# Moving the first attention step in an S5 and cross-attention layer, and joining two exponential and sine chains

## The chip, the cores and the metric

The kernel runs on one core of one Trainium2 chip. The core has a matmul engine (PE, with its weight loads shown as PEld), a vector engine (DVE), an activation engine (ACT), a general engine (POOL) and a queue that issues most DMAs (SP). The metric is the device time of one execution in microseconds (us); less is better.

## The reference

One encoder layer over 2048 tokens of width 1024 (`DEPTH = 1`, so only the S5 mixer is used). One input projection gives 512 columns for the S5 mixer and 256 for the queries of a cross-attention into 256 memory tokens; both results go through one output projection, a layer norm, a mixture of 16 experts and a second norm.

```python
proj = x @ s5_w_in[j]
mix = _s5_mixer(proj[..., :S5_WIDTH], ...)
mem_out = _memory_attention(proj[..., -MEM_WIDTH:], mem, mem_w_kv[i])
y = jnp.concatenate([mix, mem_out], axis=-1) @ w_out
x = _layer_norm(DEEPNORM_ALPHA * x + y, ln1_g[i], ln1_b[i])
moe = _hier_moe(x, ...)
x = _layer_norm(DEEPNORM_ALPHA * x + moe, ln2_g[i], ln2_b[i])
```

The S5 mixer is a diagonal complex state space model in two directions, with 32 groups of 64 states; its result goes through a GELU and a gated linear layer (GLU):

```python
step = jnp.exp(log_step[direction])[:, None]
lam_bar = jnp.exp(lam * step)                    # one token's decay and turn
b_bar = ((lam_bar - 1.0) / lam)[..., None] * bmat
bu = jnp.einsum('blgc,gpc->blgp', ug, b_bar)
_, states = lax.associative_scan(_ssm_combine, (a, bu), reverse=(direction == 1), axis=1)
y = y + jnp.real(jnp.einsum('gcp,blgp->blgc', cmat, states))
g = jax.nn.gelu(y)
return g * jax.nn.sigmoid(g @ w_glu + b_glu)
```

The cross-attention is a softmax over 256 memory tokens for 4 heads of 64.

## The kernel before

The 2048 tokens are cut into 128 chunks of 16. Inside a chunk the S5 mixer is a set of matmuls with tables made from the powers of `lam_bar`; from chunk to chunk runs a scan. The 32 groups are taken in 8 blocks of 4.

**Input projection and tables (`inproj_u`, up to about 243 us).** Sixteen token tiles are projected on PE: `pu` (S5 part) and `pq` (queries), 24 and 48 matmuls a tile. `pq` has one PSUM buffer, which ACT (L294) and DVE (L295, `OT<-pq`) empty, so PE's next `pq` waits for DVE. Beside it `s5_base` makes the token's decay and turn and their powers `PR`, `PI` for 0 to 16 tokens, on DVE and partly on POOL. `exp_m1` is a chain of 16 small DVE instructions, `sincos` one of 23; each works on 64 columns. They run for the step, for a token (`rate`, `th`) and, at the function's end, for a chunk (16 times the rate and the angle). The chunk's results `decay` and `turn` feed `scan_base`, which doubles a table of turns `E` (L649 to L671, the last doublings in three sets of 512 columns). `s5_block` then makes each block's tables on DVE (`wzi`, `wi`, `wzo`, `wo`, L580 and L581) and POOL (`wtmpi`, `wtmpo`, L576), which PE transposes (`ptw`) and multiplies (`pkk`); DVE finishes a block with `ks` (L617).

**Scans (about 229 to 334 us).** `scan(b)` runs on DVE and POOL (L690 to L695, L715), in the order of blocks 6, 7, 0 to 5; ACT copies its result to `SS` (L720). Meanwhile `kv` projects the memory and PE multiplies the chunk inputs (`pvv`).

**Outputs and attention (about 290 to 440 us).** `s5_out(b)` has for each block four pieces of PE work (`py`, L802 to L805), and after every second block four pieces of transposes (`trg`, L816), each followed by `gelu`: ACT squares (L824), DVE (L825), ACT's tanh (L826), DVE (L827, `S<-gu,trg`, which reads `trg` for the last time). `py`, `trg` and `pvv` share three PSUM buffers. Before each piece the generator yields: 4 + 8 in each pair of blocks, 48 in all. There PE may take steps of attention. A token tile of attention is three steps: scores (`pS` on PE, two PSUM buffers; DVE's maximum `nm`, L737; ACT's exponential `pe`, L740; DVE's `ri`, L742; POOL's product, L743), probabilities (`pT`, L757, emptied to `th` and `tl`) and values (`po`, L773). Steps of different tiles are interleaved, 57 in all. PE's order here is written by hand, and the table `STEPS` says how many steps go ahead of each piece. The other engines' order, and PE's elsewhere, is set by the framework's scheduler from its own estimates. Buffers of the attention and of later weights lie where those of the scan lay.

**After it:** the GLU (`gh`, `gl`, `pg`), the output projection with routing, then the experts to the end.

Of the kernel before, what the change touches and what calls it, by code (L numbers as in the profile page):

```python
# [9 lines left out]
F32 = mybir.dt.float32  # L10
# [8 lines left out]
P = 128  # L19
# [4 lines left out]
G = 32  # L24
# [26 lines left out]
SPLIT = 1024  # L51
WHOLE_T = 12
BATCHES = ((0, 4), (4, 4), (8, 2), (10, 2), (12, 2), (14, 2))
STEPS = (0,) * 8 + (1,) + (2,) * 39
ATL = (2, 3)
WIP = 3
LW = 4
# [15 lines left out]
class Kern:  # L73
# [307 lines left out]
    def s5_base(self, t0):  # L381
        nc, a = self.nc, self.a
        bp = t0.enter_context(self.pool("s5b", side="right"))
        N = 2 * G
        V = nc.vector
# [9 lines left out]
        with ExitStack() as s:  # L395
            tp = s.enter_context(self.pool("s5t", side="right"))
            n_t = [0]

            def T(nm, dt=F32):
                n_t[0] += 1  # L400

                ring = {"tag": "poly", "bufs": 3} if nm == "poly" else {}
                return tp.tile([P, N], dt, name=f"b_{nm}{n_t[0]}", **ring)

            def ts(x, s1, op0, s2=None, op1=None, dt=F32):
                o = T("ts", dt)
# [3 lines left out]
            def tt(x, y, op):  # L410
                o = T("tt")
                V.tensor_tensor(o, x, y, op=op)
                return o
# [21 lines left out]
            def exp_m1(x):  # L435
                x = ts(x, -87.0, ALU.max, 88.0, ALU.min)
                n = rnd(x, 1.4426950408889634)
                r = stt(n, -0.693145751953125, x, MUL, ADD)
                r = stt(n, -1.42860682030941723212e-6, r, MUL, ADD)
                q = horner(r, [1 / 40320., 1 / 5040., 1 / 720., 1 / 120., 1 / 24., 1 / 6., 0.5, 1.0])  # L440
                sc = ts(n, 127.0, ADD, 8388608.0, MUL, dt=I32).bitcast(F32)
                m = tt(q, sc, MUL)
                return stt(sc, -1.0, m, ADD, ADD)
# [5 lines left out]
            def sincos(th):  # L449

                n = rnd(th, 1.0 / (2 * math.pi))
                r = stt(n, -6.28125, th, MUL, ADD)
                r = stt(n, -0.0019350051879882812, r, MUL, ADD)
                r = stt(n, -(2 * math.pi - 6.28125 - 0.0019350051879882812), r, MUL, ADD)
                w = ts(r, 0.25, MUL)
                z = tt(w, w, MUL)
                sp = horner(z, [1 / 362880., -1 / 5040., 1 / 120., -1 / 6.])
                s = stt(sp, 1.0, w, ADD, MUL)
                c = ts(horner(z, [-1 / 3628800., 1 / 40320., -1 / 720., 1 / 24., -0.5]), 1.0, ADD)
                s2 = stt(s, 2.0, c, MUL, MUL)  # L460
                c2 = ts(tt(s, s, MUL), -2.0, MUL, 1.0, ADD)
                return stt(s2, 2.0, c2, MUL, MUL), stt(s2, -2.0, s2, MUL, MUL)

            step = ts(exp_m1(lst), 1.0, ADD)
            rate = tt(lre, step, MUL)
            em = exp_m1(rate)
            th = tt(lim, step, MUL)
            sf, cm = sincos(th)
            cf = ts(cm, 1.0, ADD)
            er = tt(tt(em, cf, MUL), cm, ADD)  # L470
            ei = stt(em, 1.0, sf, ADD, MUL)
            PR, PI = self.PR, self.PI
# [30 lines left out]
            for d in range(2):  # L503
                V = (nc.vector, nc.gpsimd)[d]
# [22 lines left out]
            V.tensor_tensor(self.Dd, dcol.unsqueeze(2).to_broadcast([P, NB, 16]),  # L527
                            e32.unsqueeze(1).to_broadcast([P, NB, 16]), op=MUL)

            decay = ts(exp_m1(ts(rate, 16.0, MUL)), 1.0, ADD)  # L530
            sin, cos = sincos(ts(th, 16.0, MUL))
            for par in range(2):
                r = slice(par * 64, par * 64 + 64)
                for d in range(2):
                    col = slice(d * G + par, d * G + G, 2)
                    V.tensor_copy(self.decay[r, :, d], decay[r, col])
                    V.tensor_scalar(self.turn[r, 0, :, d], cos[r, col], 1.0, None, op0=ADD)
                    V.tensor_scalar(self.turn[r, 1, :, d], sin[r, col], 1.0 - 2.0 * d, None, op0=MUL)
        self.dump("PR", self.PR)
        self.dump("PI", self.PI)  # L540
        d = self.dram
# [1065 lines left out]
```

## Time and profile before

| | |
|---|---|
| median of 3 runs | 1087.34 us |
| range | 1083.37 to 1088.72 us |
| the profiled execution | 1077.7 us |
| its span on the core | 1075.9 us |
| PE busy | 896.7 us (83%) |
| DVE busy | 825.0 us (77%) |
| ACT, POOL busy | 540.8, 537.4 us |

The span runs from the core's first to its last instruction; the execution's own time has 1.8 us around it. A share of busy time is a mean over stages with different limits, so the stages are read one by one: for each, which engine never waits, and what the other waits for. In rows of waits, the engine and line that waited stand first, then what ended the wait, then the sum, the count and the longest.

### The profile page before, as it was taken

What the parts mean: (1) busy time and instruction counts of PE and PEld (TensorE: products, weight loads), DVE (VectorE), ACT (ScalarE), POOL (GpSimd) and SP (SyncE); (2) the same over time, 40 slices, a digit from 0 to 9 for tenths busy, and PEclk for the clock granted to TensorE, in tenths of its full rate; (3) what the DMA queues carried; (4) which work ended last, traced back from release to release, by engine and by line L of the source; (5) the groups of instructions that cost most, each with busy time, mean ns of one, the idle gap of its engine ahead of it and who ended that gap; (6) DMA issues with size and microseconds to landing.
All of it is one profiled execution on the core that took longest, in us unless ns stands there. A gap on an engine that the chain in (4) does not pass through costs nothing. (4 is left out here: it accounts for less than half of the span.)

```text
span 1075.9 us, 18762 instructions
## 1 busy us (share of the span) xinstructions
PE 896.7 (83%) x7108; PEld 607.8 (56%) x7108; DVE 825.0 (77%) x1636; ACT 540.8 (50%) x1068; POOL 537.4 (50%) x379
## 2 busy tenths in 40 slices
PE   7778599986754999899999988599959996988980
PEld 4445465675643777444555557486647664755640
DVE  7999988969997676384486866379858787978874
ACT  5122253445748777477743421366636564745530
POOL 1475755426664332324946364524544566357554
PEclk9899899999886999999999996899989999999995
DMA  7113355275171422326755341675568669658431
GB/s 258 40 44 119 122 181 200 70 234 188 48 226 43 154 80 80 120 77 244 252 177 80 121 116 62 246 294 192 199 239 306 214 227 341 216 193 286 170 96 66
DMA packets 65198, 178.14 MB, mean 166 GB/s; under 512 B 15120, under 2 KB 33424, under 8 KB 57680
## 3 DMA queue, kind: packets, MB, share of 16 engines
q1 hardware_dynamic: 44800, 128.83, 36.5%
q0 software_dynamic: 20304, 48.07, 12.9%
q8 instruction: 57, 0.93, 0.4%
q14 instruction: 37, 0.30, 0.1%
HBM read 141.95 MB, written 58.49 MB: 186 GB/s over the span
## 5 line engine op out<-in xcount | busy, mean ns | idle before, releaser
L92 DVE SCALAR_TENSOR_TENSOR wl<-raw,wh 128x1024 f16<-128x1024 f32 x82 | 97.7, 1219 | 10.1 <-ACT wh L91 10.1
L91 ACT ACTIVATE wh<-raw 128x1024 f16<-128x1024 f32 x82 | 82.0, 1048 | 23.3 <-PE pg L109 12.2
L109 PE MATMUL pg<-xl,wh 128*128 128x288 f16 (+1 forms) x256 | 72.4, 285 | 5.1 <-DVE xl L1477 4.4
L108 PE MATMUL pg<-xh,wh 128*128 128x288 f16 (+1 forms) x256 | 72.8, 286 | 2.9 <-ACT xh L1476 1.8
L1221 POOL DMA_INDIRECT xs<-xg,idxall x31 | 39.4, 1272 | 71.4 <-DVE xg L1514 41.9
L108 PE MATMUL pu<-xh,wh 128*128 128x288 f16 (+1 forms) x256 | 72.1, 284 | 1.9 <-DVE hl L1063 1.9
L110 PE MATMUL pg<-xh,wl 128*128 128x288 f16 (+1 forms) x256 | 72.1, 284 | 0.5 <-issue 0.5
L110 PE MATMUL pu<-xh,wl 128*128 128x288 f16 (+1 forms) x256 | 72.0, 284 | 0.0
L109 PE MATMUL pu<-xl,wh 128*128 128x288 f16 (+1 forms) x256 | 71.9, 284 | 0.0
L109 PEld LDWEIGHTS <-wh 128*128 128x128 f16 x576 | 58.1, 101 | 20.6 <-issue 7.1
L110 PEld LDWEIGHTS <-wl 128*128 128x128 f16 x576 | 57.9, 101 | 20.0 <-issue 6.8
L108 PEld LDWEIGHTS <-wh 128*128 128x128 f16 x576 | 58.0, 101 | 19.4 <-issue 4.6
L108 PE MATMUL pq<-xh,S 128*128 128x128 f16 x256 | 50.1, 233 | 15.9 <-DVE OT L295 15.9
L743 POOL TENSOR_TENSOR pe<-pe,ri 128x1024 f32<-128x1024 f32 x16 | 30.3, 1895 | 54.5 <-DVE ri L742 40.6
L108 PE MATMUL py<-wh,hh 128*128 128x512 f16 x120 | 45.9, 384 | 13.2 <-DVE xg L1514 10.1
L1216 POOL DMA_INDIRECT xg<-x1d,idxall x31 | 39.2, 1266 | 32.6 <-DMA out_x<-xg,idxall 14.5
L108 PE MATMUL pu<-winh,xh 128*128 128x512 f16 x128 | 49.7, 389 | 6.7 <-ACT winh L91 6.6
L691 POOL TENSOR_TENSOR m<-S,R 128x1024 f32<-128x1024 f32 x10 | 31.4, 3144 | 41.7 <-DVE S L715 23.6
L110 PE MATMUL pq<-xh,S 128*128 128x128 f16 x256 | 50.3, 233 | 0.0
L109 PE MATMUL pq<-xl,S 128*128 128x128 f16 x256 | 50.1, 233 | 0.0
L1477 DVE TENSOR_TENSOR xl<-pt,xh 128x512 f16<-128x512 f32 x60 | 39.5, 682 | 13.6 <-ACT xh L1476 8.4
L109 PE MATMUL pu<-winl,xh 128*128 128x512 f16 x128 | 49.4, 386 | 0.3 <-DVE winl L92 0.3
(471 smaller groups left out, 3134.1 us busy)
## 6 DMA issues: line engine op xcount, KB each, us to landing
raw<-in_w_gate SPq DMA_DIRECT2D x16, 1024.0 KB
raw<-in_w_up SPq DMA_DIRECT2D x16, 1024.0 KB
raw<-in_w_down SPq DMA_DIRECT2D x16, 1024.0 KB
xr<-in_xT SPq DMA_DIRECT2D x16, 512.0 KB
xs<-wo SPq DMA_DIRECT2D x16, 512.0 KB
wol<-xs SPq DMA_DIRECT2D x16, 512.0 KB
M<-kd SPq DMA_DIRECT2D x64, 128.0 KB
xres<-in_x SPq DMA_DIRECT2D x16, 512.0 KB
```

The costliest lines, as they stand in the source:

```text
L91: self.nc.scalar.activation(hi, raw, AF.Copy, scale=WS)
L92: self.nc.vector.scalar_tensor_tensor(lo, raw, WS, hi, op0=ALU.mult, op1=ALU.subtract)
L108: mm(ps, lh, rh, start=first, stop=False)
L109: mm(ps, lh, rl, start=False, stop=False)
L110: return mm(ps, ll, rh, start=False, stop=last)
L691: Q.tensor_tensor(m[:, 1], S[:, :, 1::-1], tab(1), op=ALU.mult)
L743: nc.gpsimd.tensor_tensor(pe, pe, ri.unsqueeze(2).to_broadcast([P, 4, 256]), op=ALU.mult)
L1216: return self.nc.gpsimd.indirect_dma_start(out=out, out_offset=None, in_=src, in_offset=bass.IndirectOffsetOnAxis(ap=idx, axis=0))
L1221: st = self.nc.gpsimd.indirect_dma_start(out=self.xs, out_offset=bass.IndirectOffsetOnAxis(ap=si, axis=0), in_=z[:sz], in_offset=None, bou ...
L1477: nc.vector.tensor_tensor(xl[:, ds_, :n], pt, xh[:, ds_, :n], op=ALU.subtract)
```

## The change

Two edits. The table `STEPS` now has no attention step in the first 20 places and two in each of the other 28, so the first step stands ahead of the transposes of blocks 2 and 3 instead of at those of blocks 0 and 1, and the last stands at the kernel's last transposes instead of in those of blocks 4 and 5. And `s5_base` puts a token's and a chunk's rate side by side into one tile of 128 columns, their angles likewise, and runs one `exp_m1` and one `sincos` over both; the chunk's own chains at the end of the function are gone.

```diff
-STEPS = (0,) * 8 + (1,) + (2,) * 39
+STEPS = (0,) * 20 + (2,) * 28
@@ s5_base
+            wide = False
             def T(nm, dt=F32):
                 n_t[0] += 1
-                ring = {"tag": "poly", "bufs": 3} if nm == "poly" else {}
-                return tp.tile([P, N], dt, name=f"b_{nm}{n_t[0]}", **ring)
+                ring = {"tag": "poly" + "w" * wide, "bufs": 3} if nm == "poly" else {}
+                return tp.tile([P, 2 * N if wide else N], dt, name=f"b_{nm}{n_t[0]}", **ring)
...
             step = ts(exp_m1(lst), 1.0, ADD)
-            rate = tt(lre, step, MUL)
-            em = exp_m1(rate)
-            th = tt(lim, step, MUL)
-            sf, cm = sincos(th)
-            cf = ts(cm, 1.0, ADD)
+            rates = tp.tile([P, 2 * N], F32, name="rates")
+            ths = tp.tile([P, 2 * N], F32, name="ths")
+            for o, x in ((rates, lre), (ths, lim)):
+                V.tensor_tensor(o[:, 0:N], x, step, op=MUL)
+                V.tensor_scalar(o[:, N:], o[:, 0:N], 16.0, None, op0=MUL)
+            wide = True
+            ems = exp_m1(rates)
+            sfs, cms = sincos(ths)
+            cfs = tp.tile([P, 2 * N], F32, name="cfs")
+            V.tensor_scalar(cfs, cms, 1.0, None, op0=ADD)
+            wide = False
+            em, sf, cm, cf = (x[:, 0:N] for x in (ems, sfs, cms, cfs))
...
-            decay = ts(exp_m1(ts(rate, 16.0, MUL)), 1.0, ADD)
-            sin, cos = sincos(ts(th, 16.0, MUL))
             for par in range(2):
                 r = slice(par * 64, par * 64 + 64)
                 for d in range(2):
-                    col = slice(d * G + par, d * G + G, 2)
-                    V.tensor_copy(self.decay[r, :, d], decay[r, col])
-                    V.tensor_scalar(self.turn[r, 0, :, d], cos[r, col], 1.0, None, op0=ADD)
-                    V.tensor_scalar(self.turn[r, 1, :, d], sin[r, col], 1.0 - 2.0 * d, None, op0=MUL)
+                    col = slice(N + d * G + par, N + d * G + G, 2)
+                    V.tensor_scalar(self.decay[r, :, d], ems[r, col], 1.0, None, op0=ADD)
+                    V.tensor_copy(self.turn[r, 0, :, d], cfs[r, col])
+                    V.tensor_scalar(self.turn[r, 1, :, d], sfs[r, col], 1.0 - 2.0 * d, None, op0=MUL)
```

DVE has 1582 instructions instead of 1622; the other engines' counts stay (PE 12108, ACT 985, POOL 407, SP 304). Line numbers after the edit are 8 to 10 higher in `s5_base` and 8 higher below it. The scheduler also arranges many rows anew.

PE at the first transposes `trg`, before: between the first of them and the next two stand scores `pS` of tile 0 (the last four rows of it are here), and the scores of tile 1 follow.

```order
L734 LDWEIGHTS OT
L734 MATMUL pS_3527<-kh,OT 128x256
L735 LDWEIGHTS OT
L735 MATMUL pS_3527<-kl,OT 128x256
L816 MATMUL trg_3539<-ident,gt_3437 128x128 x4
L816 MATMUL trg_3549<-ident,gt_3437 128x128 x4
L734 LDWEIGHTS OT
L734 MATMUL pS_3561<-kh,OT 128x256
```

PE at the same place now: all four transposes stand together, and the outputs `py` of block 2 follow.

```order
L824 MATMUL trg_3424<-ident,gt_3355 128x128 x4
L824 MATMUL trg_3434<-ident,gt_3355 128x128 x4
L824 MATMUL trg_3444<-ident,gt_3355 128x128 x4
L824 MATMUL trg_3454<-ident,gt_3355 128x128 x4
L810 MATMUL py_3472<-M_3467,U 128x256
L811 MATMUL py_3472<-M_3467,U 128x256
L812 MATMUL py_3472<-wol_3465,SS 128x256
L813 MATMUL py_3472<-wol_3465,SS 128x256
```

Scores have moved behind 32 matmuls `py` of blocks 2 and 3 (8 of these rows are shown above in part), to the next transposes.

ACT at that place, before: `SS` of the last scan (the second row of x8), then the exponentials of tile 0.

```order
L824 ACTIVATE gu_3511<-trg_3506 128x512
L824 ACTIVATE gu_3544<-trg_3539 128x512
L826 ACTIVATE gu_3511<-gu_3511 128x512
L720 ACTIVATE SS<-S 64x2x128 x8
L740 ACTIVATE pe_3516,sm_3517<-pS_3518,nm_3523 128x256 x2
L740 ACTIVATE pe_3516,sm_3517<-pS_3527,nm_3532 128x256 x2
```

ACT now: the last scan's `SS` stands ahead of both tanh (L834), and no exponential is near.

```order
L832 ACTIVATE gu_3429<-trg_3424 128x512
L832 ACTIVATE gu_3439<-trg_3434 128x512
L728 ACTIVATE SS<-S 64x2x128 x8
L834 ACTIVATE gu_3429<-gu_3429 128x512
L834 ACTIVATE gu_3439<-gu_3439 128x512
L832 ACTIVATE gu_3449<-trg_3444 128x512
```

The first tanh has moved behind the last scan's copies.

DVE ahead of the first block's `ks`, before: of the three sets of 512 columns of `E`, one stands ahead of it (L666, L667, L670).

```order
L580 TENSOR_TENSOR wzo_680<-XC,PRb 128x512
L660 TENSOR_TENSOR E<-E,S 128x64
L295 SCALAR_TENSOR_TENSOR OT<-pq_1275,OT 64x2x128
L581 TENSOR_TENSOR wo_645<-wzo_680,wtmpo_675 128x2x256
L666 TENSOR_TENSOR S<-E 128x512
L667 TENSOR_TENSOR S<-E 128x512
L580 TENSOR_TENSOR wzi_906<-XB,PRb 128x2x240
L670 TENSOR_TENSOR E<-S 128x32x16
L581 TENSOR_TENSOR wi_902<-wzi_906,wtmpi_904 128x2x240
L617 TENSOR_TENSOR ks_724<-ks_724,Dd 128x16
```

DVE now, at the block's first `wo`: the second and third set stand there, and its `ks` comes twelve rows after the last row shown.

```order
L588 TENSOR_TENSOR wzo_586<-XC,PRb 128x512
L674 TENSOR_TENSOR S<-E 128x512
L675 TENSOR_TENSOR S<-E 128x512
L589 TENSOR_TENSOR wo_563<-wzo_586,wtmpo_584 128x2x256
L678 TENSOR_TENSOR E<-S 128x32x16
L588 TENSOR_TENSOR wzo_589<-XC,PRb 128x512
L674 TENSOR_TENSOR S<-E 128x512
L675 TENSOR_TENSOR S<-E 128x512
L589 TENSOR_TENSOR wo_563<-wzo_589,wtmpo_584 128x2x256
L678 TENSOR_TENSOR E<-S 128x32x16
```

Two sets of the scan's table have moved ahead of the first block's end.

## Rows read from the trace of the kernel before

**Rows 1.** Engine busy time by stretch: start:end, length, busy (instructions), clock, DMA.
```profile
27.00:54.00 27.00, 20.37 (x151) 13.39 (x150) 26.50 (x101) 4.60 (x8) 13.25 (x15) 0.87 0.14 40
108.00:135.00 27.00, 14.55 (x174) 11.73 (x174) 25.33 (x35) 7.54 (x19) 19.48 (x11) 0.81 0.36 122
162.00:189.00 27.00, 27.00 (x208) 15.72 (x205) 22.52 (x34) 10.13 (x25) 13.72 (x7) 1.00 0.57 203
300.00:330.00 30.00, 13.25 (x48) 9.66 (x48) 28.33 (x35) 14.67 (x35) 19.20 (x7) 0.73 0.70 209
```

**Rows 2.** PE's waits at 30 to 60, 60 to 90 and 90 to 135 us.
```profile
PE pq L108 <- DVE OT L295: 6.6, 2, 4.4
...
PE pq L108 <- DVE OT L295: 7.5, 3, 3.5
...
PE pkk L614 <- DVE wo L581: 7.2, 1, 7.2
```

**Rows 3.** DVE in order of time: start, duration, instruction, count.
```profile
20.24 0.28 DVE L527 TENSOR_TENSOR Dd<-dcol,e 128x128 f32<-128x128 f32 x1
20.44 0.22 DVE L431 SCALAR_TENSOR_TENSOR b_poly<-b_poly,b_st 128x64 f32<-128x64 f32 x1
...
35.83 0.22 DVE L417 SCALAR_TENSOR_TENSOR b_st<-b_st 128x64 f32<-128x64 f32 x1
35.97 0.22 DVE L431 SCALAR_TENSOR_TENSOR b_poly<-b_poly,b_st 128x64 f32<-128x64 f32 x1
...
36.24 0.19 DVE L407 TENSOR_SCALAR b_ts<-b_st 128x64 f32<-128x64 f32 x1
36.34 0.22 DVE L431 SCALAR_TENSOR_TENSOR b_poly<-b_poly,b_st 128x64 f32<-128x64 f32 x1
```

**Rows 4.** PE's waits from 335 to 441 us.
```profile
PE pS L734 <- ACT pe L740: 15.4, 2, 15.0
PE po L773 <- DVE tl L759: 4.5, 6, 1.6
PE trg L816 <- DVE S L827: 2.1, 1, 2.1
...
PE pT L757 <- POOL pe L743: 0.4, 1, 0.4
```

**Rows 5.** PE, then DVE, then ACT, in order of time around 330 us.
```profile
318.38 1.91 PE L816 MATMUL trg<-ident,gt 128*128 128x128 f32 x8
335.32 0.37 PE L734 MATMUL pS<-kh,OT 128*128 128x256 f16 x1 [15.02 <-ACT pe L740]
...
330.04 0.69 DVE L695 TENSOR_TENSOR S<-S 128x512 f32<-128x512 f32 x1 [1.64 <-POOL S L691]
...
336.97 0.68 DVE L827 SCALAR_TENSOR_TENSOR S<-gu,trg 128x512 f32<-128x512 f32 x1
...
330.82 3.41 ACT L720 ACTIVATE SS<-S 64x256 f32<-64x256 f32 x8 [1.76 <-DVE S L695]
334.25 0.47 ACT L740 ACTIVATE pe<-pS,nm 128x256 f32<-128x256 f32 x1
...
336.06 0.64 ACT L826 ACTIVATE gu<-gu 128x512 f32<-128x512 f32 x1
```

**Rows 6.** One tile of attention: its first score on PE, its product on POOL.
```profile
348.02 0.27 PE L734 MATMUL pS<-kh,OT 128*128 128x256 f16 x1
348.13 0.27 PE L735 MATMUL pS<-kl,OT 128*128 128x256 f16 x1
...
351.82 1.90 POOL L743 TENSOR_TENSOR pe<-pe,ri 128x1024 f32<-128x1024 f32 x1 [4.15 <-DVE ri L742]
```

**Rows 7.** Engine busy time by stretch, as in rows 1.
```profile
335.30:342.00 6.70, 5.96 (x28) 4.45 (x28) 5.79 (x11) 6.70 (x21) 1.89 (x1) 0.55 0.00 0
421.30:436.00 14.70, 14.02 (x66) 12.02 (x64) 6.08 (x11) 7.07 (x14) 0.00 (x0) 1.00 0.00 1
436.00:440.10 4.10, 2.02 (x16) 1.71 (x16) 2.57 (x4) 2.85 (x6) 0.00 (x0) 1.00 0.85 309
440.10:483.00 42.90, 41.56 (x186) 18.39 (x185) 31.07 (x40) 26.87 (x44) 16.07 (x6) 0.96 0.29 94
```

**Rows 8.** ACT, then DVE, in order of time: the GLU's first copies.
```profile
440.05 1.14 ACT L853 ACTIVATE gh<-S 128x512 f16<-128x512 f32 x2
...
440.80 1.29 DVE L854 TENSOR_TENSOR gl<-S,gh 128x512 f16<-128x512 f32 x2
```

**Rows 9.** DVE's sets of 512 columns of the table `E`, from 0 to 135 us.
```profile
L667 DVE TENSOR_TENSOR S<-E 128x512 f32<-128x512 f32 x3 | 4.8, 1594 | 0.0
L670 DVE TENSOR_TENSOR E<-S 128x512 f32<-128x512 f32 x3 | 4.7, 1575 | 0.0
L666 DVE TENSOR_TENSOR S<-E 128x512 f32<-128x512 f32 x3 | 2.6, 865 | 0.0
```

## The prediction

> **What bounds the kernel now.** The first view is the table of busy time by stretch [rows 1], since a mean over the span hides which engine sets which stage. At 27 to 54 us DVE works for 26.5 of 27.0 us and PE for 20.4; at 108 to 135 us it is 25.3 to 14.6. At 162 to 189 us PE is busy for all 27.0 us. From 300 to 330 us, in the scans, DVE has 28.3 of 30 us and PE 13.3. So the start is bound by DVE, the rest of the projection by PE, the scans by DVE with POOL. The second view is PE's waits [rows 2]: 6.6 and 7.5 us for `OT` (DVE's emptying of `pq`) between 30 and 90 us, then 7.2 us for one `wo`. Work taken from DVE there reaches PE; from about 135 us on it would not.
>
> The third view is the same one for the outputs [rows 4]: of PE's waits after 335 us nearly all is one of 15.0 us, of scores `pS` for ACT's `pe`. The timelines [rows 5] tell why: PE stops at about 320.3 us behind `trg` and resumes at 335.32; DVE's last scan ends at 330.73, ACT copies it from 330.82 to 334.23, and only then come the exponentials. This stall ends with the scan, not with attention. The last view is the outputs' later part [rows 7]: PE is busy 14.0 of 14.7 us from 421.3 to 436 us, in 32 matmuls `py` issued in two passes each, so nothing is wanting there but 0.7 us.
>
> **The joined chains.** 16 instructions of `exp_m1`, 23 of `sincos` and one addition leave DVE, 40 in all; counted in the code, 13 have one tensor operand and 27 have two. As many others grow from 64 to 128 columns. What one costs in a row of its like is the distance between two starts, which is less than its duration, since they overlap [rows 3]: 35.83 to 35.97, 0.14 us, with two operands; 36.24 to 36.34, 0.10 us, with one; 20.24 to 20.44, 0.20 us, for two operands and 128 columns. A wide one with one operand isn't in these rows; I take 0.14. Removed: 13 × 0.10 + 27 × 0.14 = 5.1 us. Grown: 13 × 0.04 + 27 × 0.06 = 2.1 us, with roundings 2.1 to 2.5; I take 2.4. Net **-2.7 us** of DVE. The bounds are 0 (the removed ones ran while DVE had to wait for others anyway) and -6 (their full durations, 0.19 and 0.22, are saved: 13 × 0.19 + 27 × 0.22 - 2.4). I take -2.7, since they follow one another in DVE's order and the starts are what that costs. DVE is the bound there, so I carry it whole to PE's stage and to the end.
>
> The full durations have a rule behind them: the Trainium skill, "VectorE: DVE Perf Modes", section "The TRN2 errata — SBUF-src ops pay a fixed extra latency per instruction", gives (N + 151)/0.96 ns for such an instruction, which exposes the latency between instructions. The 0.22 us of the rows agrees as a duration, the 0.14 us between starts does not. By the page the term would be about -6 and the time below 3.6 us lower.
>
> The scheduler also moves the second and third set of 512 columns of `E` ahead of the first block's `ks`. I cost that at nothing: PE has projections left to run while DVE makes tables. Without that cover it is the slower rival below. The other rearrangements, in the GLU, the output projection and the experts, are 0 ± 3 us: their instructions are the same, and PE leaves no long gap in the 42.9 us after 440 us, where it is busy for 41.6 [rows 7].
>
> **Attention twelve places later.** One expects the 15 us stall to go, since PE no longer stops at `pS`. I think it stays and changes its name. In order, the four `trg` now stand together, in three PSUM buffers; the fourth needs the first one's last reader, DVE's `S<-gu,trg`, which needs ACT's tanh. The order shows the last scan's eight `SS` ahead of that tanh. So: `SS` ends at 334.23, the tanh takes 0.64, DVE 0.68 [rows 5], and PE resumes at about 335.55, against 335.32: +0.2. Then 32 matmuls `py` run, as many as in 421.3 to 436 us and as closely.
>
> What was done in the stall or beside `py` now stands bare at the second set of `trg`. Between a tile's first score and the end of its product lie 348.02 to 351.82 + 1.90, 5.7 us [rows 6]. PE has to cover it: scores of tile 0 (8 × 0.11 = 0.9), a `trg` (eight of its transposes took 1.91 us ahead of the stall, where the clock was lower [rows 1, 5]; for four I take 0.5), scores of tile 1 (0.9), a `trg`: 2.8 us. Then `pT` waits. Undisturbed that is 2.9 us. But two gelus share ACT and DVE with the exponentials, two operations of 0.6 to 0.7 us on each engine for each `trg`. I take half of one gelu, **+4.1**, with bounds 2.9 and 5.6.
>
> The scores of tile 0, 0.9 us, lay in the stall; now they cost PE time: **+0.9**. Before, the first exponentials and products let PE wait another 0.4 and 0.4 us [rows 4]; those go: **-0.8**. At the end the last transposes waited 2.1 us for a gelu [rows 4], and now tiles of attention stand between them: **-2.1**. But the GLU's first copies `gh` and `gl`, 0.57 and 0.64 us [rows 8], now stand behind the last values and a tanh: 0.64 + 0.57 + 0.64, **+1.9**. Last, the clock. At 436 to 440.1 us PE was busy for 2.0 of 4.1 us, and the next 42.9 us show a granted clock of 0.96 [rows 7]: 1.7 us of full speed lost behind a thin stretch. The new start-up is a thin stretch too; I take half, **+0.8**, between 0 and 1.7. The first 6.7 us after the stall run at 0.55 in any case.
>
> Sum: +0.2 + 4.1 + 0.9 - 0.8 - 2.1 + 1.9 + 0.8 = **+5.0 us**, from +1 to +9 by the bounds.
>
> **The sum.** -2.7 + 5.0 = +2.3 us. Against the profiled execution, 1077.7 us (span 1075.9 and 1.8 around it), that is 1080.0; the median of the runs is 9.6 us higher, and on it the forecast is 1087.3 + 2.3 = **1089.6 us**. By the table of bounds it goes from 1083 to 1096.
>
> **Rivals.**
> *The start-up is covered.* Attention's first scores could run while DVE and ACT are free, since ACT works 7.1 and DVE 6.1 of the 14.7 us before [rows 7]. Then PE's waits of 0.7 and 2.1 us in 435 to 440 us go, and nothing is added: 1087.3 - 2.7 - 2.8 = 1081.8 us. Against it: PE takes its order as written, and `pS` stands behind a `trg` of the same set. A rule that speaks for it: the Trainium skill, "Perfetto Trace Analysis", section "Optimization Strategy", says that interleaving stages with different bounds may improve a kernel.
>
> *The early waits vanish.* If PE's 14.1 us for `OT` [rows 2] come from DVE's order and the new order ends them, 14.1 us go and attention costs 5.0: 1078.2 us. Against it: DVE, the bound, has only 2.7 us less work.
>
> *The stall is filled.* If PE ran the 32 matmuls `py` inside the 15 us, about 14 us would go: 1087.3 - 2.7 - 14.0 + 5.0 = 1075.6 us. It needs the fourth `trg` free before the scan's end, so a tanh ahead of `SS`. ACT's order shows the opposite.
>
> *Slower: the scan's table starves PE.* Two of three sets of `E` now stand ahead of the first block's end: (4.8 + 4.7 + 2.6) × 2/3 = 8.1 us of DVE [rows 9]. If PE has no projection left in front of that block's transposes and `pkk`, it waits that long: 1087.3 + 8.1 + 2.3 = 1097.7 us. It decides as soon as PE's queue ahead of the first `pkk` is shorter than DVE's; the 7.2 us for `wo` [rows 2] say that it was so once already. Against it: the same sets have to be made anyway, so DVE gets them back before 135 us, and PE's projections wait less.
>
> **How the numbers follow.** The forecast has 0.50, the slower rival 0.20, the covered start-up 0.15, the early waits 0.10, the filled stall 0.05. About 0.5%, 5.4 us, is what a measurement of this kernel can tell from no change: below 1081.9 is faster, above 1092.8 slower. The forecast's own spread puts 0.03 of it below and 0.21 above. Faster: 0.50 × 0.03 + half of the covered start-up, 0.07, + nearly all of the early waits and the filled stall, 0.13, gives 0.21. Slower: 0.50 × 0.21 + 0.20 × 0.85, and a little more, gives 0.28. The rest, 0.51, is the same. The range of 1079 to 1098 leaves out most of the early waits and the filled stall and a little at the top.
>
> **What the profile would show.** Right: PE's wait of some 15 us at 320 us is now of `trg` for DVE's `S`; behind it 32 `py` without a wait; about 14 us later `pT` waits some 4 us for POOL's `pe` or `pS` for ACT; at the end `pg` waits some 2 us for `gl`. DVE's busy time is about 40 × 0.2 us less in the sum of durations, and the projection ends some 2.7 us earlier. Wrong: PE's longest wait at 320 us is much below 15 us (filled stall); the waits for `OT` are gone (early waits); or a wait of 5 us or more for the first blocks' tables or `pkk` is new (the scan's table). If the projection ends later than at 243 us, the joined chains did not bring what they removed.

## The result and the profile after

| | before | after |
|---|---|---|
| median of 22 runs each | 1084.3 us | 1088.93 us |
| lowest and highest | 1074.47 to 1089.8 | 1083.25 to 1097.16 |
| the profiled execution's span | 1075.9 | 1088.5 |

The ratio is 1.0051, with a 95% interval of 1.0032 to 1.0071: on 1084.3 us that is 5.5 us slower, between 3.5 and 7.7 (the medians themselves are 4.6 us apart). The forecast was +2.3 us and 1089.6 us. That 1088.9 us comes so close to 1089.6 is luck, since two errors cancel: the difference is about twice the one forecast, and the 22 runs of before have a median 3 us below that of the three runs it was built on.

The single profiles are 12.6 us apart, more than the runs. So the trace is cut at events that both kernels have: the end of the last `pkk`, the end of the last `SS`, the start of the first `pg`, the end of the last `pg<-gl` (the last but one matmul of the GLU), the end of the last `poo`, the end. The lengths between them, in us, with a second profile of the changed kernel (after, again):

| | to last `pkk` | to last `SS` | to first `pg` | to last `pg` | to last `poo` | rest |
|---|---|---|---|---|---|---|
| before | 218.8 | 115.5 | 105.9 | 44.7 | 152.1 | 438.9 |
| after | 215.8 | 116.1 | 110.8 | 50.4 | 152.9 | 442.6 |
| after, again | 216.5 | 116.4 | 108.2 | 50.5 | 151.1 | 441.6 |

The projection gives 3.0 and 2.3 us, attention takes 4.9 and 2.3, the GLU takes 5.6 and 5.7. The last column goes from 437 to 446 us over all the kernels of this study in no order that the edits explain, so nothing is read from it. The one profile of before is of a fast execution: 1077.7 us, 6.6 us below the median of its 22 runs, while the two of the changed kernel (1090.6 and 1086.1 us) are 1.7 us above and 1.9 us below theirs. What is held against it can come out some us too large.

First, as in [rows 1], the stretches of the start and of the scans (length, then busy time with instructions for PE, PEld, DVE, ACT and POOL, the granted clock, and DMA).

```profile
27.00:54.00 27.00, 20.76 (x160) 12.93 (x159) 26.09 (x81) 4.97 (x9) 14.65 (x19) 0.94 0.14 39
108.00:135.00 27.00, 20.35 (x220) 15.68 (x218) 24.32 (x40) 11.28 (x28) 14.51 (x8) 0.94 0.49 164
300.00:330.00 30.00, 13.39 (x50) 9.97 (x48) 29.47 (x32) 18.47 (x44) 20.00 (x8) 0.70 0.75 223
```

DVE still bounds the first stretch (26.1 of 27 us), with fewer instructions (81 against 101). From 108 to 135 us PE now does 20.4 us of work where it did 14.6: it is ahead. The scans are as full as they were.

PE's waits between 312 and 470 us (what waited, what ended it, sum, count, longest), to be held against [rows 4]:

```profile
PE trg L824 <- ACT gt L815: 10.4, 2, 9.7
PE trg L824 <- DVE S L835: 7.6, 1, 7.6
PE pg L108 <- ACT sg L870: 6.0, 1, 6.0
PE po L781 <- DVE tl L767: 3.8, 4, 1.9
PE pS L742 <- ACT pe L748: 2.3, 2, 1.3
PE pg L108 <- DVE bglu L855: 1.2, 1, 1.2
PE pT L765 <- POOL pe L751: 0.8, 1, 0.8
```

The wait of 15.0 us for `pe` has become one of 9.7 for `gt` and one of 7.6 for a gelu. The third row is new, and no step of the prediction has it. The timelines of PE, ACT and DVE around the stall (start, duration, instruction, count, and in brackets the idle time before it and what ended it), against [rows 5]:

```profile
323.03 2.82 PE L824 MATMUL trg<-ident,gt 128*128 128x128 f32 x12 [9.70 <-ACT gt L815]
333.40 1.09 PE L824 MATMUL trg<-ident,gt 128*128 128x128 f32 x4 [7.55 <-DVE S L835]
...
320.66 1.70 ACT L728 ACTIVATE SS<-S 64x256 f32<-64x256 f32 x4 [7.50 <-POOL S L703]
322.38 0.60 ACT L815 ACTIVATE gt<-py 128x512 f32<-128x512 f32 x1
...
328.48 3.41 ACT L728 ACTIVATE SS<-S 64x256 f32<-64x256 f32 x8 [1.48 <-DVE S L703]
331.91 1.15 ACT L834 ACTIVATE gu<-gu 128x512 f32<-128x512 f32 x2
...
332.57 1.28 DVE L835 SCALAR_TENSOR_TENSOR S<-gu,trg 128x512 f32<-128x512 f32 x2 [2.99 <-ACT gu L834]
```

Both waits are ACT's order. A copy of `gt` that was ready stands behind an `SS` that waits 7.50 us for POOL, and both tanh stand behind the last scan's `SS`. PE goes on 1.5 us after that scan's `SS`, against 1.1 us before.

The start-up, on PE and POOL, against [rows 6]:

```profile
351.91 0.27 PE L742 MATMUL pS<-kh,OT 128*128 128x256 f16 x1
...
354.35 0.27 PE L742 MATMUL pS<-kh,OT 128*128 128x256 f16 x1 [0.96 <-ACT pe L748]
...
356.26 0.34 PE L742 MATMUL pS<-kh,OT 128*128 128x256 f16 x1 [1.32 <-ACT pe L748]
...
358.87 1.97 PE L765 MATMUL pT<-ident,pe 128*128 128x128 f32 x8 [0.78 <-POOL pe L751]
...
356.92 1.89 POOL L751 TENSOR_TENSOR pe<-pe,ri 128x1024 f32<-128x1024 f32 x1 [27.41 <-DVE ri L750]
```

From the first score to the first `pT` are 6.96 us, with 3.1 us of waits in them. Last, the GLU, ACT's rows of after with PE's resumption, then two ACT rows of before:

```profile
456.80 1.06 ACT L91 ACTIVATE owh<-oraw 128x1024 f16<-128x1024 f32 x1 [1.82 <-DMA oraw<-in_w_out]
463.10 1.06 ACT L102 ACTIVATE owh<-oraw 128x1024 f16<-128x1024 f32 x1 [5.24 <-DMA oraw<-in_w_out]
464.06 0.67 ACT L870 ACTIVATE sg<-pg,bglu 128x512 f32<-128x512 f32 x1
...
464.78 0.59 PE L108 MATMUL pg<-gh,E 128*128 128x512 f16 x1 [6.04 <-ACT sg L870]
```

```profile
454.52 1.25 ACT L862 ACTIVATE sg<-pg,bglu 128x512 f32<-128x512 f32 x2
...
461.57 1.04 ACT L102 ACTIVATE owh<-oraw 128x1024 f16<-128x1024 f32 x1
```

`pg` has six PSUM buffers. After six groups PE needs the first one back, which `sg` (the GLU's tanh) frees. Before, two `sg` stand ahead of the fifth conversion of the out weights, `owh<-oraw`. After, the fifth stands ahead of the first `sg` and waits 5.24 us for its transfer; PE waits 6.04 us with it.

### The profile page after: what moved, and what is told of

Its sections match the earlier page's. It is cut to its first block, busy times and chain, and to the rows that moved or that the text cites. A ratio compares the mean times of both kernels' runs of the same rounds, so it can differ in the third digit from the quotient of the medians.

```text
span 1088.5 us, 18744 instructions
## 1 busy us (share of the span) xinstructions
PE 904.0 (83%) x7108; PEld 612.2 (56%) x7108; DVE 821.5 (75%) x1596; ACT 541.1 (50%) x1068; POOL 538.0 (49%) x379
## 5 line engine op out<-in xcount | busy, mean ns | idle before, releaser
L1229 POOL DMA_INDIRECT xs<-xg,idxall x31 | 35.4, 1142 | 74.8 <-DVE xg L1522 35.6
L108 PEld LDWEIGHTS <-wh 128*128 128x128 f16 x576 | 57.9, 101 | 16.8 <-issue 2.7
L108 PE MATMUL pq<-xh,S 128*128 128x128 f16 x256 | 49.5, 231 | 15.5 <-DVE OT L295 15.4
L108 PE MATMUL py<-wh,hh 128*128 128x512 f16 x120 | 47.6, 397 | 12.8 <-DVE xg L1522 9.3
L1522 DVE SCALAR_TENSOR_TENSOR xg<-py,idxall,xg 128x512 f32<-128x512 f32 x60 | 43.1, 744 | 19.8 <-DMA xg<-xs,idxall 15.1
L1224 POOL DMA_INDIRECT xg<-x1d,idxall x31 | 36.3, 1172 | 39.2 <-DMA out_x<-xg,idxall 21.4
L699 POOL TENSOR_TENSOR m<-S,R 128x1024 f32<-128x1024 f32 x10 | 35.2, 3520 | 37.7 <-DVE S L723 21.5
L584 POOL TENSOR_TENSOR wtmpo<-YC,PI 128x1024 f32<-128x1024 f32 x16 | 33.4, 2089 | 32.6 <-DVE wi L589 26.9
```

What stands on the lines that cost most here:

```text
L108: mm(ps, lh, rh, start=first, stop=False)
L584: Q.tensor_tensor(t[:, :, 0:n], ch(y, all_, n), pw(self.PI, lo, d, all_, n), op=ALU.mult)
L699: Q.tensor_tensor(m[:, 1], S[:, :, 1::-1], tab(1), op=ALU.mult)
L1224: return self.nc.gpsimd.indirect_dma_start(out=out, out_offset=None, in_=src, in_offset=bass.IndirectOffsetOnAxis(ap=idx, axis=0))
L1229: st = self.nc.gpsimd.indirect_dma_start(out=self.xs, out_offset=bass.IndirectOffsetOnAxis(ap=si, axis=0), in_=z[:sz], in_offset=None, bou ...
L1522: nc.vector.scalar_tensor_tensor(xg[:sz, hs], py[:sz], gate, xg[:sz, hs], op0=ALU.mult, op1=ALU.add, **acc)
```

## The experiments

Every ratio is to runs of the kernel before on the same chip. The first four ran together on one chip, the next four on a second, and the last four on a third.

**Each edit alone, and the first hold of the GLU.**

The kernel before with the new table, and the changed kernel with the old one:

```diff
-STEPS = (0,) * 8 + (1,) + (2,) * 39
+STEPS = (0,) * 20 + (2,) * 28
```

```diff
-STEPS = (0,) * 20 + (2,) * 28
+STEPS = (0,) * 8 + (1,) + (2,) * 39
```

> The kernel before with the new table of steps alone. Theory: the step table carries the whole loss, in two places. Attention's start-up lies bare (4 to 5 us between the last scan's copies and the first pg), and in the GLU ACT takes the fifth owh<-oraw, which waits for its transfer, ahead of the first sg, so that the third token tile's pg waits some 6 us for sg. Sum +8 to +11 us against before. Rival: the loss comes from the new order of the early tables (the joined chains); then this kernel is within 3 us of before and has no wait of pg for sg. Second rival: the 6 us wait of pg was one execution's accident; then +4 to +5 us.

> The joined chains alone, with the old table of steps. Theory: DVE has about 2.5 us less to do where it is the bound, the last scan's copies end 2 to 3 us earlier, the GLU's order is as before (two sg ahead of the fifth owh): -2 to -3 us against before. Rival (the moved sets of the table E starve PE): the projection ends later and the kernel is 2 us or more slower. Rival (the gain is lost on the way): within 1 us, with the projection's end earlier and the scans' end not.

The steps alone: 1.0135 (1.0101 to 1.0170), +14.5 us, more than the 8 to 11 expected. Up to the last `poo` its profile is 10.9 us behind before, of which 5.7 lie in the GLU, with the same wait of 6.0 us for `sg`, 2.6 in attention and 1.5 ahead of the last `pkk`, where the table edits nothing. This settles where that wait comes from: the table of steps, not the chains. The rivals fall.

The chains alone: 1.0031 (1.0009 to 1.0053), +3.3 us and not -2 to -3. The last `pkk` ends at 215.7 us and the last `SS` at 332.0, 3.0 and 2.2 us earlier, as expected, so the table `E` starves nobody. But attention takes 109.1 us instead of 105.9. PE's waits in it, then ACT's rows in the scans:

```profile
PE trg L824 <- ACT gt L815: 11.5, 2, 10.8
...
PE pS L742 <- ACT pe L748: 4.6, 2, 4.2
```

```profile
322.02 1.69 ACT L728 ACTIVATE SS<-S 64x256 f32<-64x256 f32 x4 [8.65 <-POOL S L703]
323.74 0.60 ACT L815 ACTIVATE gt<-py 128x512 f32<-128x512 f32 x1
```

The changed kernel with a first hold:

```diff
-                (self.split_w_q if c in OWQ else self.split_w)(wh[:, c], wl[:, c], raw)
+                with self.tc.issue_after(self.sg) if c >= 4 else ExitStack():
+                    (self.split_w_q if c in OWQ else self.split_w)(wh[:, c], wl[:, c], raw)
```

`self.sg` is here the second `sg` of the first token tile; the edge sets the order on ACT alone and waits for nothing.

> The changed kernel, in which the fifth and sixth conversion of the out weights may be issued only after the second sg of the first token tile. Theory: the wait of pg for sg (6.0 us) is the order of ACT's rows and goes, and nothing else needs the fifth chunk so early: 4 to 6 us faster than the changed kernel, that is -1 to +2 us against before. Rival: the out weights become late, the first poo waits for owh or owl as long as pg waited; then as slow as the changed kernel, about +5 us.

A miss: 1.0091 (1.0063 to 1.0119), the GLU takes 51.5 us, and the wait for `sg` has grown to 7.5 us. ACT's rows:

```profile
458.53 1.25 ACT L870 ACTIVATE sg<-pg,bglu 128x512 f32<-128x512 f32 x2
463.78 1.06 ACT L102 ACTIVATE owh<-oraw 128x1024 f16<-128x1024 f32 x1 [4.00 <-DMA oraw<-in_w_out]
466.56 1.06 ACT L91 ACTIVATE owh<-oraw 128x1024 f16<-128x1024 f32 x1 [1.73 <-DMA oraw<-in_w_out]
467.53 0.61 ACT L874 ACTIVATE mh<-sg 128x512 f16<-128x512 f32 x1
```

Two `sg` are early now, but the third needs a buffer that `mh` frees, and `mh` stands behind both conversions.

**The first step at place twelve (`start12`).**

```diff
-STEPS = (0,) * 20 + (2,) * 28
+STEPS = (0,) * 12 + (2,) * 36
```

> The changed kernel with the first attention step twelve places in, behind the transposes of blocks 0 and 1 and ahead of the outputs of block 2, so that 1.7 us of py stand between two steps while the first exponentials are made. Theory: the start-up is hidden under py, PE waits under 1 us for pe there, the end is as before, and so is the GLU's order: -1 to -4 us against before. Rival (the loss is not the start-up but all that moved later): +3 us or more.

A miss: 1.0040 (1.0007 to 1.0072), +4.3 us, as the rival has it. The waits for `pe` at the start are gone and the GLU takes 44.3 us, but attention takes 114.2 us. In PE's waits from 312 to 445 us the gelu's second wait at the last transposes is back (9.6 us in two, the longest 7.5), there are ten waits for `tl`, and the first `pg` waits 3.1 us for the last gelu. Between 316 and 440 us the lower level of the clock, 1.2 GHz, is granted for 30.7 us, against 21.9 in before, and 33.5 and 20.5 in the two profiles of the changed kernel.

```profile
PE trg L824 <- DVE S L835: 9.6, 2, 7.5
PE po L781 <- DVE tl L767: 6.9, 10, 1.3
```

**The changed kernel again, a second hold, and the order of `gt`.**

> The changed kernel itself, beside the other three on one chip. Theory: +3.5 to +8 us against before, as measured already, with the scans ending about 2 us earlier, attention 3 to 5 us longer and the GLU 5 to 6 us longer (a wait of pg for sg). Rival: on the chip of the single changes, where the steps alone cost 14.5 us and the chains alone 3.3 us, the two together cost more, +10 us or above.

1.0051 (1.0028 to 1.0075), 5.5 us by the ratio and 4.7 between the medians: the first measurement repeats. The steps alone lost more, but on another chip, where before ran at 1076.4 us. There the first hold, whose GLU takes only 1.1 us longer than the changed kernel's, cost 1.0091, so part of the gap may be the chip's; what the chips do to it is open.

```diff
-                with self.tc.issue_after(self.sg) if c >= 4 else ExitStack():
+                with self.tc.issue_after(self.half) if c >= 4 else ExitStack():
```

`self.half` is the second `mh` of the first token tile.

> The changed kernel with the fifth and sixth conversion of the out weights behind the second mh of the first token tile, and not only behind its second sg. Theory: the first hold only moved the wait from the first sg to the third, since the third needs a buffer that mh empties, and mh stood behind the fifth conversion; now pg waits under 1.5 us for sg in the GLU, which takes 44 to 46 us from the first to the last pg in place of 50.4: 4 to 6 us faster than the changed kernel. Rival: the wait is paid elsewhere (the first poo waits for owh), and the time stays.

1.0032 (1.0002 to 1.0062): by the ratios 2 us better than the changed kernel beside it, with intervals that overlap, and half of what was expected. PE still waits 4.0 us for the third `sg`, which stands behind the held conversions, and the GLU takes 47.6 us. Held behind the fourth `sg`, as in all four last runs, it takes 43.7 to 45.2 us, as in before.

Then the chains alone, with an order edge from the last `gt` of block 1 (`cp`) to every `SS` of block 4 (`self.ssi[4]`):

```diff
+            for si in self.ssi[4] if (b, gp) == (1, 1) else ():
+                self.tc.add_manual_dep(si.ins, cp.ins.name, mybir.DependencyInfo(
+                    mybir.DependencyClass.NoSync, mybir.DependencyReason.DATA), reason="order")
```

> The joined chains alone, in which ACT may copy the eighth scan's neighbour, the scan of block 4, to SS only after the last gt of block 1, as the kernel before does by itself. Theory: what the joined chains win (2 to 3 us at the scans' end) is lost because the last gt stands behind an SS that waits 8.7 us for POOL; with the rows in the old order the first trg starts near 315 us in place of 324, attention takes 106 us from the scans' end to the first pg in place of 109, and the kernel is 2 to 3 us faster than the chains alone, that is about as fast as before or up to 2 us faster. Rival: the wait of trg costs nothing, since the scans' end is what is waited for; then as the chains alone.

0.9987 (0.9960 to 1.0014): the time comes out as expected, but against the chains alone on another chip, and the mechanism does not come out. `trg` starts at 314.7 us, yet attention takes 109.5 us, no less than with the chains alone: the waits for `gt` and `pe` have become one of 16.8 us that ends with the last scan. PE resumes 1.1 us after the last `SS` here (332.81 to 333.89 us) as with the chains alone (332.01 to 333.10): the earlier `trg` gains nothing, as the rival has it.

```profile
PE pS L745 <- ACT pe L751: 16.8, 1, 16.8
```

What takes longer is the time after it. Stretches of attention in this kernel and in before, as in [rows 1]:

```profile
354.00:440.00 86.00, 81.13 (x750) 68.67 (x747) 54.30 (x102) 60.44 (x173) 23.98 (x13) 0.96 0.30 95
```

```profile
354.00:440.00 86.00, 77.59 (x742) 65.60 (x740) 55.19 (x104) 60.90 (x174) 22.74 (x12) 1.00 0.33 102
```

The granted clock is 0.96 against 1.00, which is 3.4 us of full speed in 86 us. So the theory that the row of `gt` eats the chains' gain falls. All stages of the two kernels agree within 1 us (215.7, 116.3, 109.1, 44.5, 153.6 and 438.9 us for the chains alone, 216.6, 116.3, 109.5, 44.6, 153.7 and 439.2 here), so that the ratios 1.0031 and 0.9987, from two chips, are no measure of this edge. That these clock falls would be the whole reason for the longer attention is not shown: they differ between executions of one program too (17.6 and 7.8 us at the lower level between the last `SS` and the first `pg` in the two profiles of the changed kernel).

**The place alone (`place_held`).** The changed kernel with `gt` ahead as above and the GLU held behind the fourth `sg`, the gelu left behind the last scan.

> The changed kernel with the last gt of block 1 ahead of the scan of block 4 and the GLU's order held (behind the fourth sg), the gelu left behind the last scan. Theory: what is left against before is the place of attention and the chains: -2.5 us at the scans' end, +2 to +5 us from there to the first pg, the GLU within 1.5 us of before: 0 to +3 us against before. Rival: the GLU's lost time moves to the out projection, then +5 us as the changed kernel.

1.0014 (0.9982 to 1.0046), +1.5 us, as the theory has it, with an interval from -1.9 to +5.0 that also holds no change. The last `SS` ends 1.3 us earlier than in before, attention takes 111.5 us, +5.6, and the GLU 45.2 us, +0.4. PE waits 17.8 us in one piece for the gelu behind the last scan. With the GLU in order the time agrees with the prediction's +2.3, as far as this interval can tell. Against the changed kernel (1.0051 twice) it is 4 us better, with intervals that overlap: the GLU's 5.6 us are shown by the lengths and by the wait, less sharply by the whole time.

**Filling the stall (`dve_early`).** If both waits are ACT's and DVE's order, the four gelu of blocks 0 and 1 can be put ahead of the last scan. Order edges (no waits) go from the gelu's tanh to the `SS` of blocks 4 and 5, and from its products to the scan and the turn of block 5; the GLU is held as in the second hold, and `gt` is held ahead by the edge shown above.

```diff
+        if nm[0] == "0":
+            for si in self.ssi[4] if nm[1] in "01" else self.ssi[5]:
+                self.tc.add_manual_dep(si.ins, th.ins.name, mybir.DependencyInfo(
+                    mybir.DependencyClass.NoSync, mybir.DependencyReason.DATA), reason="order")
...
+            for si in self.scans[5] if nm[1] in "01" else self.turns[5]:
+                self.tc.add_manual_dep(si.ins, st.ins.name, mybir.DependencyInfo(
+                    mybir.DependencyClass.NoSync, mybir.DependencyReason.DATA), reason="order")
```

`nm` is the gelu's name (block pair and piece), `th` its tanh, `st` its last product; `scans` and `turns` are DVE's scan and second turn of a block.

> The changed kernel with the four gelu of blocks 0 and 1 ahead of the last scan's work on DVE and ACT (and the GLU's order held as in the run above). Theory: the stall of PE ends with the scans only because the fourth trg waits for a tanh and a product that stand behind the last scan; taken ahead, PE does the 32 py of blocks 2 and 3 while the last scan runs, the scans end some 5 us later (eight products of 0.68 us on DVE), which nothing waits for, and the first scores start near 343 us in place of 352: 6 to 10 us faster than the changed kernel beyond the GLU's 5, 4 to 10 us faster than before. Rival: DVE is the bound and the 5 us that go into the scans push everything behind them; then no gain over the GLU's.

0.9927 (0.9896 to 0.9958), 7.9 us faster than before and 13 us than the changed kernel, with the GLU's and `gt`'s order in the 13. PE, then DVE:

```profile
315.02 1.53 PE L834 MATMUL trg<-ident,gt 128*128 128x128 f32 x12 [0.69 <-ACT gt L822]
324.90 1.09 PE L834 MATMUL trg<-ident,gt 128*128 128x128 f32 x4 [8.35 <-DVE S L849]
...
322.70 1.27 DVE L843 SCALAR_TENSOR_TENSOR gu<-gu,trg 128x512 f32<-128x512 f32 x2
324.07 1.29 DVE L849 SCALAR_TENSOR_TENSOR S<-gu,trg 128x512 f32<-128x512 f32 x2
325.27 2.63 DVE L725 TENSOR_TENSOR_SCAN S<-decay,S 128x128 f32<-128x128 f32 x8
```

PE goes on at 324.9 instead of 333.4 us, does the 32 `py` beside the last scan, and starts the scores at 343.0 instead of 351.9. The last `SS` comes 6.5 us later, at 338.4 us, and nothing waits for it. The rival falls: DVE is the bound of the scans, but it is not PE's bound if PE has work that the last scans don't feed.

The next two put two of the products ahead of the turn of block 4 as well, and hold the GLU behind the fourth `sg`; the second also starts attention at place sixteen. The third is the first without the joined chains.

```diff
-            for si in self.ssi[4] if nm[1] in "01" else self.ssi[5]:
+            for si in self.ssi[4]:
...
-            for si in self.scans[5] if nm[1] in "01" else self.turns[5]:
+            for si in self.turns[4] if nm[1] in "01" else self.scans[5]:
```

The second, besides:

```diff
-STEPS = (0,) * 20 + (2,) * 28
+STEPS = (0,) * 16 + (2,) * 32
```

> As the run with the four gelu taken ahead (0.993 of before), but two of them now ahead of the turn of the scan of block 4, and all ahead of the last scan, on DVE; and the fifth and sixth out weights behind the fourth sg of the first token tile. Theory: in that run the first product waited until 322.7 us behind the scan of block 4, though the transposes were ready at 316.5; now the fourth trg starts near 320 in place of 324.9, which takes 4 to 5 us more off, and the GLU's wait of 3.5 us falls under 1.5 us: 12 to 16 us faster than before, ratio 0.985 to 0.990. Rival: from here PE waits for what DVE gives back later (SS of block 4 or 5 for its py, the first scores), so that it stays at 0.993.

> The run above with the first attention step four places earlier, in the outputs of block 3, so that py stands between the first scores and the first pT. Theory: the start-up, for which the changed kernel pays 3 us of waits and some thin clock, is hidden, and attention still ends inside the last transposes: 2 to 4 us faster than the run above. Rival: as with the first step at place twelve, what is won at the start is paid back at the end, where fewer steps lie between the last transposes, and by DVE, which must share the scans' end with the exponentials: same as the run above or up to 4 us slower.

> The first run of this set without the joined chains. Theory: both orders being held, it shows what the joined chains are worth alone: the scans' end, and the whole, 2 to 3 us later than in the first run, ratio to it about 1.002. Rival: the joined chains are worth nothing or cost time, since the table E moves ahead of the first block's tables: equal to or faster than the first run.

The first: 0.9940 (0.9906 to 0.9974). It differs from the run of the place alone, on the same chip at 1.0014, by the gelu's order and nothing else: that order is worth 8.0 us. The wait for the gelu falls from 8.4 to 5.6 us and the last `poo` ends 2.4 us earlier than in the run above, but no gain over it can be measured; the time that was expected (0.985 to 0.990) is missed. The rival holds: a wait for `gt` is new, whose copy now stands behind the last scan's `SS`, and the second set of `trg` starts at 341.5 us, only 1.0 us earlier than above.

```profile
341.50 0.66 PE L834 MATMUL trg<-ident,gt 128*128 128x128 f32 x4 [3.00 <-ACT gt L822]
```

Attention at place sixteen (`early2_s16`): 1.0008 (0.9979 to 1.0037), 7 us lost against the first, more than the rival has. Its waits, and the cause on ACT:

```profile
PE trg L834 <- DVE S L849: 7.9, 2, 5.9
PE pS L749 <- ACT pe L755: 7.7, 2, 7.3
...
PE pg L108 <- DVE S L849: 3.1, 1, 3.1
```

```profile
337.21 3.41 ACT L732 ACTIVATE SS<-S 64x256 f32<-64x256 f32 x8
340.63 0.47 ACT L755 ACTIVATE pe<-pS,nm 128x256 f32<-128x256 f32 x1
```

The exponentials stand behind the last scan again, and at the end the last gelu are bare again (3.1 us). The start-up is not hidden by an earlier place, it is tied to the scan again.

Without the joined chains: 0.9888 (0.9848 to 0.9929), 12 us faster than before and the lowest ratio of all, in six runs. Its projection ends at 219.0 us in place of 216.4, as it should, but its last `SS` ends within 0.2 us of the first run's and its first `pg` 1.5 us earlier. Of the 6.0 us between the medians of the two, the profiles show 1.2 up to the last `poo`; the rest lies in the last stage, where nothing is read. The intervals of the two overlap, so a loss by the joined chains is not shown; a gain of 2.7 us is not there either.

## Why the prediction was right or wrong

**What bounds the kernel** was read rightly: the stall at 320 us ends with the last scan and attention has no part in it. `dve_early` shows more: it ends there by the order of ACT and DVE, and with another order PE goes on 8.5 us earlier. "Nearly all" of PE's waits is too much, though: the 15.0 us are part of 24.1 after 335 us, and the other 9.1 lie in attention, whose sum counts only some of them.

**The joined chains.** The prices hold. The rows of DVE in after, in order of time, as in [rows 3]:

```profile
29.45 0.21 DVE L409 TENSOR_SCALAR b_ts<-b_st 128x128 f32<-128x128 f32 x1
29.59 0.28 DVE L433 SCALAR_TENSOR_TENSOR b_poly<-b_poly,b_st 128x128 f32<-128x128 f32 x1
29.79 0.28 DVE L414 TENSOR_TENSOR b_tt<-b_ts 128x128 f32<-128x128 f32 x1
```

A wide one with one operand costs 0.14 us from start to start, with two 0.20, as taken. The last `pkk` ends 3.0 and 2.3 us earlier (predicted 2.7). Over all profiles it ends at 215.2 to 218.1 us in the eleven with the joined chains and at 218.8 to 220.3 in the three without; the means are 2.8 us apart. An estimate from the formula of the Trainium skill, "VectorE: DVE Perf Modes", section "The TRN2 errata — SBUF-src ops pay a fixed extra latency per instruction", would have it at some 6 us. The measurement decides for the distance between starts, and the formula fits the duration alone: 0.29 us for 128 columns, where the rows have 0.28. What failed is "I carry it whole to PE's stage and to the end". At the last `SS` 2.4 and 1.4 us are left, and the chains alone were no faster. DVE's waits for POOL between 216 and 330 us, in before and in after:

```profile
DVE S L695 <- POOL m L691: 2.2, 1, 2.2
```

```profile
DVE S L703 <- POOL m L699: 6.7, 3, 2.2
```

Two more waits of 2.2 us stand in the scans of every kernel here with the joined chains (one more in `dve_early`) and in none without them: part of DVE's gain turns into waiting for POOL, 0.6 and 0.9 us of it up to the last `SS`. What takes the rest between the scans and the end is open, and with before's one profile as the measure it may not be lost at all: 0.9987 has room for it, 1.0031 has not.

**The stall changes its name and stays** was right: 17.3 us of waits in two pieces, against 15.0 [rows 5] and 4.7 for `gt` in before, and PE resumes 0.4 us later after the last `SS` than before, +0.2 predicted.

**The start-up** was sized at 6.9 us from the first score to the first `pT`; it is 6.96. It is 6.95 or 6.96 in every kernel here that starts attention at place twenty, so PE's own work does not set it; `pT` starts when POOL's product is done. Half of one gelu was a guess that came out. Of the 4.1 us of exposed waiting 3.1 are waits of PE, 3.9 in the second profile, where PE works less slowly. From 351.4 to 364.5 us PE is busy for 10.0 of 13.1 us at a mean granted clock of 0.74, and the lower level holds from 356.3 to 363.2. At the end the first `pg` waits 1.2 us for `bglu`, a small row behind the last gelu on DVE, not 1.9 for `gl`. The sum of this part, +5.0, stands against +4.9 and +2.3 in the two profiles and +5.6 in `place_held`. But the +4.9 is met by luck. From PE's resumption to the first `pg`, in before, after and after again, as in [rows 1]:

```profile
335.30:440.10 104.80, 95.36 (x876) 79.85 (x875) 69.38 (x130) 76.48 (x221) 30.32 (x16) 0.97 0.30 94
```

```profile
333.40:442.60 109.20, 100.11 (x884) 84.54 (x884) 68.61 (x129) 75.77 (x220) 30.29 (x16) 0.93 0.29 83
```

```profile
334.30:441.00 106.70, 96.09 (x884) 81.36 (x884) 68.77 (x129) 75.60 (x220) 30.32 (x16) 0.97 0.29 85
```

PE is idle for 9.4, 9.1 and 10.6 us: the waits grow by -0.3 and +1.2 us, where the prediction's terms for them (4.1 - 0.8 - 2.1 + 1.9) say +3.1. It left out that PE's waits for `tl` and `th`, 5.5 us in before, would fall to 3.8 and 4.1. In the first profile most of the +4.9 is the clock, sized at 0.8: PE is busy 4.7 us longer at 0.93 for 0.97, which the second profile does not repeat. Nor do the lengths show that the place costs anything: with the old place the chains alone and with `gt` take 109.1 and 109.5 us for attention, and the six profiles with the new place and the stall 108.2 to 111.5.

**The step that failed** is "the other rearrangements ... are 0 ± 3 us", argued from "PE leaves no long gap". That PE leaves no gap in before says what the order of before does, not that the next order leaves none. The GLU measured +5.6 and +5.7 us. The row that told it was there ahead of the run: in ACT's order the fifth `owh<-oraw` stands ahead of the first `sg`. I read the order at the places that the edit touches, and not 100 us later, where the scheduler had also chosen anew. The 1083 to 1096 us "by the table of bounds" hold the bounds of the chains and of attention alone, without these ±3. With +5.6 the sum is +7.9, where the runs say 5.5 and at most 7.7. The 2.4 us between are not settled: the chains' gain, partly lost on the way, would add to the sum, and the waits in attention, 1.9 to 3.4 us below their terms, would take from it.

**The rivals.** The sets of `E` starve PE: the first `ks` is indeed 9.5 us later (101.5 to 111.0 us), but PE has projections to run until then, and the projection ends earlier; it falls. The early waits for `OT` vanish: in the whole projection 15.4 us of them are left of 15.9, with one of 7.2 among them; it falls. The start-up is covered: it falls for the place chosen, and `start12` and `early2_s16` show that an earlier place doesn't cover it either. Of the Trainium skill's rule for it, "Perfetto Trace Analysis", section "Optimization Strategy", both sides are seen: outputs interleaved with the scans won 8 us (0.9940 against 1.0014), attention interleaved with them as well lost 7 (1.0008). The filled stall had 0.05 and was rejected by ACT's order, rightly for this kernel. As a mechanism it is the one that pays when the order is changed: 0.9927, 0.9940 and 0.9888.

**The chances.** The time is slower by just over 0.5%, for which 0.28 stood; 0.51 stood on no change.

## What to carry to other kernels

Where a scheduler places rows by its estimates, an edit changes the order in stages that it doesn't touch, so read the new order of every in-order engine for one pattern: a row that waits for a transfer or another engine, standing ahead of a ready row that frees a buffer. Here one such row cost 6 us, and two tanh behind the last scan's copies cost a gain of 8 us. A stall that "ends with the scan" is only bound by the scan if PE has no work that the scan doesn't feed; ask what stands between PE and that work, and whether it has to stand there. A saving on the bound engine is worth its size only as far as the next engine that it has to wait for.

## What the runs showed of the hardware that was not expected

Two executions of one program had the clock's lower level for 17.6 and 7.8 us in the same stage, after the same order of instructions; at half speed that is at most 4.9 us of work, and the stage was 2.5 us longer, which a single profile would put down to the edit. A hold that names the wrong row can make a wait longer: behind the second `sg` it went from 6.0 to 7.5 us, behind the second `mh` to 4.0, and behind the fourth `sg` to 2.9 us in three pieces.
